# Two half products ordered by row block, attention's own bank marked free a tick later, and GpSimd's last sum moved ahead of its last power

## The chip, the cores and the metric

The kernel runs on one core of a Trainium2 chip. Its time is the device time of one execution in microseconds (us); several executions are timed, and their median counts. A profiled execution is taken beside them, and its trace is what the views below are read from. Engines are named as in the profile: PE is TensorE's matmul, PEld its weight load, DVE is VectorE, ACT is ScalarE, POOL is GpSimd, SP is SyncE, which here only issues transfers.

## The reference

Two decoder layers on 512 rows of 1024 features, in float32. The even layer projects its input into retention heads and an RG-LRU branch, gates both, and maps them back. The odd layer, where the change lies, is differential attention with 8 heads:

```
q, k, v, g = split(h @ w_in);  q, k = rope(q), rope(k)        # two maps a head
p   = softmax(masked q k^T)                                   # by blocks of 128 rows
out = (p[map 0] - lam * p[map 1]) @ v                         # 256 columns a head
out = out * rsqrt(mean(out^2) + eps) * subln_g * (1 - lambda_init) * silu(g)
y   = out @ w_out
h   = layer_norm(alpha * h + y)
```

The result of that last layer norm is the output.

## The kernel before

The 512 rows are four row blocks of 128. Every float32 operand is held as two parts, high and low (`split`: ScalarE rounds the high part, VectorE subtracts it), and every product is three matmuls (`mm3`, line 155: high by high, low by high, high by low) into the same bank of PSUM. Weights come as pieces of 128 x 1024 through `fetch` (line 170): SP issues the load into one of a few raw buffers, ScalarE and VectorE split it into one of five slots of `wsp`. `take(ahead)` (line 191) hands out the next piece and first fetches up to `ahead` pieces beyond it, so a later `take` is also what puts later loads into the program. A slot is free again when PE has read its old piece for the last time, and the cast of the piece five places on waits for that.

**Order.** PE and SP run in program order, as the code is written. The order of DVE, ACT and POOL is planned by the framework from its own estimate of times, with priorities (`tc.high_priority`); a few instructions are pinned by `tc.keep_in_program_order`. Each engine then takes its instructions strictly in that order.

**Ticks.** The attention of a head and row block is a generator (`attention`, line 684) that is mixed into other matmul work by a small planner, `Side` (line 54). After each step of three matmuls the surrounding unit calls `side.tick()`; a tick advances `now` by one and runs at most one piece of one due job, looking at no more than the first three attention jobs in order. A piece ends with `yield n`, due again n ticks later. The pieces of a block are: scores of both maps with their exponentials (`as`, `e`); transposes of the weights into `wt`; the value product into `po` (rows `po<-ov..`), followed by ACT's squares, POOL's sum and power and DVE's `o`; transposes of `o` into the second half of the same bank (rows `L740`), whose copy by ACT and DVE into `om<head>h` and `om<head>l` empties the bank. The waits between them are `ATT_SCORES` (7 or 8 ticks), `ATT_TURN` (3 or 4) and `ATT_NORM` (5), each one more while `busy[0]` is set, in the combined units.

**The bank of the value product.** There is one own bank (`ps_av`). `av[0]` holds the tick from which it counts as free:

```
if own:
    av[0] = side.now + ATT_FREE
```

with `ATT_FREE` = 2, set when the transposes of `o` are issued. In query and key units (`spare[0]` true) a block may instead borrow one of the four banks of the projections (`ps_pj`), once in 8 ticks. Elsewhere it waits for its own bank. If PE reaches a bank that is not emptied yet, PE waits.

**The units of the odd layer** (list `od`, line 307): values and gates of the first two heads, query and key units of heads 0 to 2, then for group g = 1 to 3 a combined unit of gates and values (`gates_values`, line 816), an output unit (`odd_out`, for two heads that are done), and query and key units; at the end the output unit of heads 6 and 7 with the last layer norm. The order is combined unit 1, output of heads 0 and 1, queries and keys of heads 3 and 4, combined unit 2, output of heads 2 and 3, and so on.

**The combined unit** computes gates and values of two heads from 2 x 2 blocks with seven half products instead of eight. A half product (`product`, line 823) covers two row blocks n = 0, 1 (one bank each) and four pieces of the inner dimension kt = 0 to 3, which lie in two weight pieces: eight steps. Its loops run over the weight piece, then the row block, then the two kt of that piece, so a bank gets two steps, the other two, the first two again, and the other the last two. The first half product goes into the banks `one`, the second into `two` (`gv<g>a` and `gv<g>b` in the trace). `copies` (line 834) then copies `one` to SBUF, `gate` (line 840) adds `two` to the copy on DVE. When the unit starts, some of the four banks have just been used by the query and key units or were lent to attention.

**The end.** `layer_norm` (line 397) of row block 2 is `late`: its second half goes over ACT and POOL, in pieces that `odd_end` (line 880) starts through `rest()` while block 3's output is computed. POOL's multiplication is followed by its addition (line 424), which at present is issued from within block 3's norm, right behind its `rsqrt` (the power at line 395) by the hook `then()`. SP sends each half row block out when it is done.

Of the kernel before, what the change touches and what calls it, by code (L numbers as in the profile page):

```python
# [11 lines left out]
ALU = mybir.AluOpType  # L12
# [91 lines left out]
def trunk(ctx: ExitStack, tc: tile.TileContext, a):  # L104
# [38 lines left out]
    def cut(t, *ix):  # L143
        return t[0][ix], t[1][ix]
# [249 lines left out]
    def rsqrt(var, out):  # L394
        nc.gpsimd.tensor_tensor(out=out, in0=var, in1=nhalf[:, :1], op=ALU.pow)  # L395

    def layer_norm(y, sb, gb, late=False, src=None, then=lambda: None):
        hv = [y[:, sb, hf * HALF:hf * HALF + HALF] for hf in range(2)]
        src = [hv[0], src or hv[1]]
        st = stats.pop(sb, None)  # L400
        if st is None:
            st = small.tile([P, 2, 6], F32, tag="bst", name="bst", bufs=2)
            for hf in range(2):
                nc.vector.bn_stats(out=st[:, hf], in_=hv[hf])
        mv = small.tile([P, 2], F32, tag="bmv", name="bmv", bufs=2)
        nc.vector.bn_aggr(out=mv, in_=st)
        rs = small.tile([P, 1], F32, tag="lrs", name="lrs", bufs=2)
        ve = small.tile([P, 1], F32, tag="rs", name="lve")
        nc.vector.tensor_scalar(out=ve, in0=mv[:, 1:2], scalar1=EPS, scalar2=None, op0=ALU.add)  # L409
        rsqrt(ve, rs)  # L410
        then()
        if late:


            nc.vector.scalar_tensor_tensor(out=hv[0], in0=hv[0], scalar=mv[:, 0:1], in1=gb[0][0], op0=ALU.subtract, op1=ALU.mult)
            yield
            nm = small.tile([P, 1], F32, tag="lnm", name="lnm", bufs=1)
            tc.keep_in_program_order(nc.vector.tensor_scalar(out=nm, in0=mv[:, 0:1], scalar1=rs, scalar2=-1.0, op0=ALU.mult, op1=ALU.mult))
            nc.scalar.activation(out=hv[1], in_=hv[1], func=AF.Identity, scale=rs, bias=nm)
            nc.gpsimd.tensor_tensor(out=hv[1], in0=hv[1], in1=gb[0][1], op=ALU.mult)  # L420
            yield
            tc.keep_in_program_order(nc.vector.scalar_tensor_tensor(out=hv[0], in0=hv[0], scalar=rs, in1=gb[1][0], op0=ALU.mult, op1=ALU.add))
            yield 0, hv[0]
            tc.keep_in_program_order(nc.gpsimd.tensor_tensor(out=hv[1], in0=hv[1], in1=gb[1][1], op=ALU.add))
            yield 1, hv[1]
            return
        for hf in range(2):
            nc.vector.scalar_tensor_tensor(out=hv[hf], in0=src[hf], scalar=mv[:, 0:1], in1=gb[0][hf], op0=ALU.subtract, op1=ALU.mult)
        for hf in range(2):
            nc.vector.scalar_tensor_tensor(out=hv[hf], in0=hv[hf], scalar=rs, in1=gb[1][hf], op0=ALU.mult, op1=ALU.add)  # L430
            yield hf, hv[hf]
# [252 lines left out]
    def attention(hd, qb, q, k, m):  # L684
# [57 lines left out]
            split(pm.rearrange("p (i s) -> p i s", s=P), cut(m, ALL, ALL, slice(qb * P, qb * P + P)))  # L742

        if own:
            av[0] = side.now + ATT_FREE

    oj, om, vs, vt, av = {}, {}, {}, {}, [0]

# [67 lines left out]
    def gates_values(i):  # L816
        def block(r, c):
            return lambda kt, n: cut(h, ALL, 4 * c + kt, slice((2 * r + n) * P, (2 * r + n) * P + P))

        def total(k):  # L820
            return lambda kt, n: tuple(sx[:, k, x, kt, n * P:n * P + P] for x in range(2))

        def product(ps, left, start, then=lambda: None):
            for j in range(2):
                if j:
                    then()
                w = take(3)
                for n in range(2):
                    for kt in range(2 * j, 2 * j + 2):
                        c = kt % 2 * HALF  # L830
                        mm3(ps[n], left(kt, n), cut(w, ALL, slice(c, c + HALF)), start and kt == 0, kt == KT // 2 - 1, skip_group_check=not start)
                        side.tick()

        def copies(ps, name, ts):

            for n in range(2):
                ts.append(work(f"{name}{i}{n}"))
                tc.keep_in_program_order(nc.scalar.copy(out=ts[n], in_=ps[n]))

        def gate(ps, ts, r):  # L840
            g = gp.tile([P, 2, S], F32, tag="g", name=f"og{i}{r}")
            for n in range(2):
                for hd in (2 * i - 2, 2 * i - 1):
                    side.need(oj[hd, 2 * r + n])
                gates[2 * r + n, i] = g[:, n]
            for n in range(2):
                nc.vector.tensor_tensor(out=g[:, n], in0=ps[n], in1=ts[n], op=ALU.add)
                silu2(g[:, n], g[:, n], ts[n])

        busy[0] = ATT_BUSY  # L850
        one = [bank(ps_pj, "pj", f"gv{i}a{n}") for n in range(2)]
        two = [bank(ps_pj, "pj", f"gv{i}b{n}") for n in range(2)]
        p1, u, p7, low = [], [], [], []
        product(one, block(0, 0), True)
        copies(one, "p1", p1)
        product(two, block(0, 1), True)
        gate(two, p1, 0)
        product(one, total(0), False)
        copies(one, "u", u)
        product(two, total(1), True, lambda: load_sum(0, 0))  # L860
        copies(two, "p7", p7)
        product(one, total(0), False, lambda: load_sum(3, 1))
        past(i - 1)
        for n in range(2):
            nc.vector.scalar_tensor_tensor(out=p7[n], in0=one[n], scalar=-1.0, in1=p7[n], op0=ALU.mult, op1=ALU.subtract)
            low.append(pair(vp, [P, S], "v", f"ov{i}{2 + n}"))
            split(p7[n], low[n])
        product(two, block(1, 1), False)
        gate(two, u, 1)
        product(one, total(1), False)  # L870
        for n in range(2):
            t = pair(vp, [P, S], "v", f"ov{i}{n}")
            nc.scalar.activation(out=t[0], in_=one[n], func=AF.Identity, scale=-1.0)
            nc.vector.scalar_tensor_tensor(out=t[1], in0=one[n], scalar=-1.0, in1=t[0].bitcast(F32), op0=ALU.mult, op1=ALU.subtract)
            vs.setdefault(i, []).append(t)
        vs[i] += low
        vt[i] = side.now + GV_VALUE
        busy[0] = 0

    def odd_end(sb):  # L880
        nonlocal rest
        last = sb == SB - 1
        norm = layer_norm(y, sb, gb1, sb == SB - 2, residual.get(1) if last else None, (lambda: rest()) if last else (lambda: None))

        def steps():
            for t in norm:
                if t is not None:
                    nc.sync.dma_start(out=a["out"][sb, :, t[0] * HALF:t[0] * HALF + HALF], in_=t[1])
                if sb == SB - 2:
                    yield  # L890

        if sb == SB - 2:
            it = steps()
            next(it)
            rest = lambda: next(it, None)
        else:
            for _ in steps():
                pass

    def past(g):  # L900
        if g >= 0:
# [160 lines left out]
```

## Time and profile before

| | |
|---|---|
| median of the timed runs | 919.15 us (918.99 to 919.6, three runs) |
| profiled execution | 919.45 us, its span 917.7 us |
| granted TensorE clock, mean | 0.998 |
| PE busy | 905.8 us, 99% |
| DVE, ACT, POOL busy | 718.1, 517.6, 113.1 us |
| DMA | 152.93 MB, mean 167 GB/s |

The span runs from the first to the last instruction; the rest of the profiled execution's time lies around it. Times in rows are us from the start of the span. In a timeline row stand the start, the duration, the engine, the line, the operation, the output tile and its inputs, the shape, a count, and in brackets the idle time before it with what ended it. Matmul ends are modelled, so distances between the starts of matmuls say more than their durations. In a row of windows stand the stretch, its length, and the busy time and count of each engine, then clock, DMA share and GB/s.

### The profile page before, as it was taken

The page shows a single profiled execution, that of the slowest core. Times are in us where ns is not written, and L with a number is a line of the kernel's source. Part 1 is how long each engine was busy: PE and PEld are TensorE (multiplying, and loading weights), DVE is VectorE, ACT ScalarE, POOL GpSimd, SP SyncE. Part 2 cuts the span into 40 slices and gives each one's busy share as a digit, 9 for nine tenths or more (in the row PEclk, how much of TensorE's full clock was granted, in tenths as well). Part 3 has the DMA queues.
Part 4 walks back from the last instruction along what each step waited for, and adds up shares of the span by engine and source line. Part 5 has one row for each costly group of instructions (what it writes and reads, how often), then busy time and mean ns, then how long its engine had stood idle before and what let it go on. Part 6 is the DMA issues. An engine that isn't in the chain of part 4 may idle for free.

```text
span 917.7 us, 11876 instructions
## 1 busy us (share of the span) xinstructions
PE 905.8 (99%) x4258; PEld 750.6 (82%) x4258; DVE 718.1 (78%) x1191; ACT 517.6 (56%) x846; POOL 113.1 (12%) x190
## 2 busy tenths in 40 slices
PE   9999999999999999999999999999999999999996
PEld 7888887888888888888888878888888888888885
DVE  5887977958868998897868887748877668867687
ACT  5567787546575668533456666435655355665440
POOL 2311010110102010010101120000120100201112
PEclk9999999999999999999999999999999999999999
DMA  8985463872829471434842226646247382178102
GB/s 288 283 278 149 125 186 91 245 203 58 263 78 270 113 205 51 169 129 149 326 179 70 69 70 229 229 161 252 70 136 250 142 321 92 58 265 276 45 1 92
DMA packets 46524, 152.93 MB, mean 167 GB/s; under 512 B 6145, under 2 KB 6273, under 8 KB 45697
## 3 DMA queue, kind: packets, MB, share of 16 engines
q1 hardware_dynamic: 41472, 135.39, 41.5%
q0 software_dynamic: 4992, 16.78, 9.5%
q8 instruction: 33, 0.54, 0.2%
q14 instruction: 27, 0.21, 0.1%
HBM read 139.57 MB, written 37.75 MB: 193 GB/s over the span
## 4 chain that ended last, share of the span: by engine, by line
PE 87%; DVE 6%; ACT 3%; issue 2%; POOL 1%; DMA 1%; SPq 0%; DVEq 0%; ACTq 0%; POOLq 0%
PE oo_ps L157 8%; PE gr_ps L157 5%; PE out_ps L157 4%; PE q_ps L157 4%; PE gl_ps L157 4%; PE ev_ps L157 4%; PE k_ps L157 4%; PE xb_ps L157 4%; PE po L157 3%; PE as L157 3%; PE ov_ps L157 2%; PE gv3a L157 2%; PE gv2a L157 2%; PE eo_ps L157 2%; PE og_ps L157 2%; PE gv3b L157 2%
## 5 line engine op out<-in xcount | busy, mean ns | idle before, releaser
L697 ACT ACTIVATE e<-as,nm 128x128 f32<-128x128 f32 (+3 forms) x64 | 33.2, 524 | 33.5 <-DVE nm L694 33.3
L704 POOL TENSOR_SCALAR zr<-z 128x1 f32<-128x1 f32 x32 | 16.4, 511 | 248.1 <-ACT e L697 248.1
L736 DVE SCALAR_TENSOR_TENSOR o<-po,ars,og 128x256 f32<-128x256 f32 x32 | 15.5, 484 | 35.0 <-POOL ars L395 35.0
L186 POOL DMA_DIRECT2D t<-t x24 | 19.2, 799 | 160.3 <-DMA t<-in_od_w 157.7
L733 POOL TENSOR_SCALAR ave<-ss,zr 128x1 f32<-128x1 f32 x32 | 16.4, 512 | 141.2 <-ACT po L730 135.2
L186 POOL DMA_DIRECT2D t<-in_od_w x24 | 19.1, 796 | 117.9 <-DMA t<-in_od_w 117.8
L694 DVE CUSTOM_DVE_ANT_0 as<-as,mask 128x128 f32<-128x128 f32 (+3 forms) x64 | 30.4, 506 | 2.3 <-PE as L157 2.3
L730 ACT ACTIVATE po<-po 128x256 f32<-128x256 f32 x32 | 11.9, 371 | 24.6 <-PE po L157 24.4
L575 DVE TENSOR_TENSOR xbp<-xbp,xc 128x512 f32<-128x512 f32 x8 | 5.5, 692 | 17.5 <-ACT xbp L572 17.5
L395 POOL TENSOR_TENSOR ars<-ave,nhalf 128x1 f32<-128x1 f32 x32 | 18.8, 587 | 2.7
L705 DVE SCALAR_TENSOR_TENSOR e<-e,zr,e 128x128 f32<-128x128 f32 (+3 forms) x32 | 17.6, 549 | 0.8
L558 DVE SCALAR_TENSOR_TENSOR xc<-xbp,vecs,xc 128x509 f32<-128x509 f32 (+2 forms) x24 | 17.8, 744 | 0.2
L395 POOL TENSOR_TENSOR lrs<-lve,nhalf 128x1 f32<-128x1 f32 x8 | 7.3, 912 | 83.1 <-DVE lve L409 83.1
L514 DVE TENSOR_TENSOR rsd<-rs,dec 128x512 f32<-128x512 f32 (+3 forms) x32 | 15.5, 484 | 2.1 <-PE rs L157 1.9
L278 DVE TENSOR_TENSOR y<-oo_ps,y 128x512 f32<-128x512 f32 x23 | 15.3, 685 | 2.2 <-PE oo_ps L157 2.1
L567 ACT ACTIVATE t<-pr,vecs 128x512 f32<-128x512 f32 x8 | 5.5, 688 | 17.5 <-PE pr L157 17.4
L709 PE MATMUL wt<-ident,e 128*128 128x128 f32 x80 | 13.9, 272 | 0.0
L152 ACT CAST hh<-ht 128x512 fp32r<-128x512 f32 x8 | 4.7, 588 | 15.5 <-PE ht L654 15.5
L709 PEld LDWEIGHTS wt<-ident,e 128*128 128x128 f32 x80 | 10.5, 140 | 3.4
L583 ACT ACT_TABLE_LOAD x8 | 10.3, 1283 | 4.2 <-DVE xc L582 4.1
L702 DVE RECIPROCAL zr<-z 128x1 f32<-128x1 f32 x32 | 5.2, 162 | 9.6 <-ACT e L697 9.4
L697 ACT ACTIVATION_READ_ACCUMULATOR e<-as,nm 128x1 f32 x64 | 12.5, 195 | 0.0
(2844 smaller groups left out, 3478.0 us busy)
## 6 DMA issues: line engine op xcount, KB each, us to landing
w_r<-in_od_w SPq DMA_DIRECT2D x58, 512.0 KB, 5.9
w_r<-in_ev_w SPq DMA_DIRECT2D x47, 512.0 KB, 5.1
t<-in_od_w SPq DMA_DIRECT2D x48, 256.0 KB, 5.5
sx<-sd SPq DMA_DIRECT2D x24, 512.0 KB, 5.7
w_r<-t SPq DMA_DIRECT2D x24, 512.0 KB, 3.3
w_r<-in_ev_wo SPq DMA_DIRECT2D x16, 512.0 KB, 4.5
w_r<-in_od_wo SPq DMA_DIRECT2D x16, 512.0 KB, 4.7
t<-in_od_w POOLq DMA_DIRECT2D x24, 256.0 KB, 5.2
```

What stands on the lines that cost most here:

```text
L157: nc.tensor.matmul(out=out, lhsT=l[n == 2], rhs=r[n == 1], start=start and n == 0, stop=stop and n == 2, **kw)
L186: nc.gpsimd.dma_start(out=dst, in_=two, max_dma_last_dim=4 * D, accum_op=ALU.add)
L395: nc.gpsimd.tensor_tensor(out=out, in0=var, in1=nhalf[:, :1], op=ALU.pow)
L514: nc.vector.tensor_tensor(out=s[:, :n], in0=ps[:, :n], in1=dec[:, :n], op=ALU.mult)
L558: nc.vector.scalar_tensor_tensor(out=xc[:, sh:], in0=xb[:, :S - sh], scalar=conv_w(w, c), in1=xc[:, sh:], op0=ALU.mult, op1=ALU.add)
L694: nc.vector.tensor_tensor_reduce(out=ps[:, :n], in0=ps[:, :n], in1=mask[:, S - n:], scale=-QK_SCALE, scalar=3.0e38, op0=ALU.add, op1=ALU.m ...
L697: nc.scalar.activation(out=e, in_=ps[:, :n], func=AF.Exp, scale=-1.0, bias=nm, accum_out=z[:, mp:mp + 1])
L704: nc.gpsimd.tensor_scalar(out=zr[:, 1:2], in0=z[:, 0:1], scalar1=z[:, 0:1], scalar2=EPS, op0=ALU.mult, op1=ALU.mult)
L705: nc.vector.scalar_tensor_tensor(out=ee[0], in0=ee[1], scalar=zr[:, 0:1], in1=ee[0], op0=ALU.mult, op1=ALU.add)
L709: nc.tensor.transpose(out=pt[:, kb * P:kb * P + P], in_=ee[0][:, kb * P:kb * P + P], identity=ident)
L733: nc.gpsimd.tensor_scalar(out=ve, in0=ss, scalar1=zr[:, 1:2], scalar2=None, op0=ALU.add)
L736: nc.vector.scalar_tensor_tensor(out=o, in0=po[:, :2 * P], scalar=rs, in1=gates[qb, hd // 2][:, hc:hc + 2 * P], op0=ALU.mult, op1=ALU.mult)
```

## The change

In `gates_values` the first two half products get `apart=True`: both weight pieces are taken first, and then all four steps of row block 0 are issued before those of row block 1. The number of steps, ticks and matmuls is the same.

In `attention` the own bank counts as free one tick later (3 instead of 2) when the transposes are issued outside query and key units.

In `layer_norm` POOL's addition follows its multiplication at once, before block 3's norm begins; the hook `then` is gone, and `odd_end` sends both halves of block 2 one after the other.

```
--- before.py
+++ after.py
@@ -394,7 +394,7 @@
     def rsqrt(var, out):
         nc.gpsimd.tensor_tensor(out=out, in0=var, in1=nhalf[:, :1], op=ALU.pow)
 
-    def layer_norm(y, sb, gb, late=False, src=None, then=lambda: None):
+    def layer_norm(y, sb, gb, late=False, src=None):
         hv = [y[:, sb, hf * HALF:hf * HALF + HALF] for hf in range(2)]
         src = [hv[0], src or hv[1]]
         st = stats.pop(sb, None)
@@ -408,7 +408,6 @@
         ve = small.tile([P, 1], F32, tag="rs", name="lve")
         nc.vector.tensor_scalar(out=ve, in0=mv[:, 1:2], scalar1=EPS, scalar2=None, op0=ALU.add)
         rsqrt(ve, rs)
-        then()
         if late:
 
 
@@ -418,11 +417,10 @@
             tc.keep_in_program_order(nc.vector.tensor_scalar(out=nm, in0=mv[:, 0:1], scalar1=rs, scalar2=-1.0, op0=ALU.mult, op1=ALU.mult))
             nc.scalar.activation(out=hv[1], in_=hv[1], func=AF.Identity, scale=rs, bias=nm)
             nc.gpsimd.tensor_tensor(out=hv[1], in0=hv[1], in1=gb[0][1], op=ALU.mult)
+            nc.gpsimd.tensor_tensor(out=hv[1], in0=hv[1], in1=gb[1][1], op=ALU.add)
             yield
             tc.keep_in_program_order(nc.vector.scalar_tensor_tensor(out=hv[0], in0=hv[0], scalar=rs, in1=gb[1][0], op0=ALU.mult, op1=ALU.add))
-            yield 0, hv[0]
-            tc.keep_in_program_order(nc.gpsimd.tensor_tensor(out=hv[1], in0=hv[1], in1=gb[1][1], op=ALU.add))
-            yield 1, hv[1]
+            yield from enumerate(hv)
             return
         for hf in range(2):
             nc.vector.scalar_tensor_tensor(out=hv[hf], in0=src[hf], scalar=mv[:, 0:1], in1=gb[0][hf], op0=ALU.subtract, op1=ALU.mult)
@@ -742,7 +740,7 @@
             split(pm.rearrange("p (i s) -> p i s", s=P), cut(m, ALL, ALL, slice(qb * P, qb * P + P)))
 
         if own:
-            av[0] = side.now + ATT_FREE
+            av[0] = side.now + ATT_FREE + (not spare[0])
 
     oj, om, vs, vt, av = {}, {}, {}, {}, [0]
 
@@ -820,7 +818,16 @@
         def total(k):
             return lambda kt, n: tuple(sx[:, k, x, kt, n * P:n * P + P] for x in range(2))
 
-        def product(ps, left, start, then=lambda: None):
+        def product(ps, left, start, then=lambda: None, apart=False):
+            if apart:
+
+                ws = [take(3) for _ in range(2)]
+                for n in range(2):
+                    for kt in range(KT // 2):
+                        c = kt % 2 * HALF
+                        mm3(ps[n], left(kt, n), cut(ws[kt // 2], ALL, slice(c, c + HALF)), kt == 0, kt == KT // 2 - 1)
+                        side.tick()
+                return
             for j in range(2):
                 if j:
                     then()
@@ -851,9 +858,9 @@
         one = [bank(ps_pj, "pj", f"gv{i}a{n}") for n in range(2)]
         two = [bank(ps_pj, "pj", f"gv{i}b{n}") for n in range(2)]
         p1, u, p7, low = [], [], [], []
-        product(one, block(0, 0), True)
+        product(one, block(0, 0), True, apart=True)
         copies(one, "p1", p1)
-        product(two, block(0, 1), True)
+        product(two, block(0, 1), True, apart=True)
         gate(two, p1, 0)
         product(one, total(0), False)
         copies(one, "u", u)
@@ -879,23 +886,18 @@
 
     def odd_end(sb):
         nonlocal rest
-        last = sb == SB - 1
-        norm = layer_norm(y, sb, gb1, sb == SB - 2, residual.get(1) if last else None, (lambda: rest()) if last else (lambda: None))
+        norm = layer_norm(y, sb, gb1, sb == SB - 2, residual.get(1) if sb == SB - 1 else None)
 
         def steps():
             for t in norm:
-                if t is not None:
+                if t is None:
+                    yield
+                else:
                     nc.sync.dma_start(out=a["out"][sb, :, t[0] * HALF:t[0] * HALF + HALF], in_=t[1])
-                if sb == SB - 2:
-                    yield
-
-        if sb == SB - 2:
-            it = steps()
-            next(it)
-            rest = lambda: next(it, None)
-        else:
-            for _ in steps():
-                pass
+
+        it = steps()
+        rest = lambda: next(it, None)
+        rest()
 
     def past(g):
         if g >= 0:
```

## The prediction

> **What bounds the kernel now.** I read the page first, then the waits of TensorE (PE), then windows, then timelines around each place that the change touches.
>
> ```profile
> span 917.7 us, 11876 instructions
> PE 905.8 (99%) x4258; PEld 750.6 (82%) x4258; DVE 718.1 (78%) x1191; ACT 517.6 (56%) x846; POOL 113.1 (12%) x190
> ...
> PE 87%; DVE 6%; ACT 3%; issue 2%; POOL 1%; DMA 1%; SPq 0%; DVEq 0%; ACTq 0%; POOLq 0%
> ```
>
> PE is busy for 99% of the span and carries 87% of the chain that ended last. Its matmul work is not changed in number, so only two things can move the time: moments in which PE stands still, and the tail after its last matmul. The waits of PE, the rows that lie where the change works:
>
> ```profile
> PE gv1a L157 <- DVE om1l L153: 0.4, 1, 0.4
> ...
> PE po L157 <- DVE om1l L153: 0.2, 1, 0.2
> ...
> PE po L157 <- DVE om4l L153: 0.2, 1, 0.2
> ```
>
> They are tenths of a microsecond each. Idle time understates them, because a matmul's modelled end lies after the start of the next one; so I size every stall by the distance between starts. The whole stake of the change is a few such stalls, in a kernel where 0.2% (about what a measurement of this kernel can tell from no change) is 1.84 us.
>
> **Part 1, the first two half products block by block.** The windows that hold exactly these two products, for groups 1, 2 and 3, with the same 82 or 81 matmuls and transposes in each:
>
> ```profile
> 532.33:548.90 16.57, 15.95 (x82) 12.74 (x81) 13.32 (x29) 10.49 (x23) 3.81 (x6) 1.00 0.20 65
> 657.37:672.74 15.37, 15.37 (x82) 12.89 (x80) 13.29 (x29) 11.26 (x24) 5.54 (x6) 1.00 0.21 69
> 780.74:796.11 15.37, 15.37 (x81) 12.89 (x80) 13.30 (x29) 11.26 (x24) 5.54 (x6) 1.00 0.21 69
> ```
>
> Group 1 takes 1.20 us more than the other two. The timeline of PE shows where:
>
> ```profile
> 533.25 0.39 PE L157 MATMUL gv1a<-w84l,hh 128*128 128x512 f32 x1
> 533.47 0.39 PE L157 MATMUL gv1a<-w84h,hl 128*128 128x512 f32 x1
> 534.27 0.50 PE L157 MATMUL gv1a<-w84h,hh 128*128 128x512 f32 x1 [0.41 <-DVE om1l L153]
> 534.61 0.40 PE L157 MATMUL gv1a<-w84l,hh 128*128 128x512 f32 x1
> ...
> 542.71 0.40 PE L157 MATMUL gv1b<-w86h,hl 128*128 128x512 f32 x1
> 543.31 0.51 PE L157 MATMUL gv1b<-w86h,hh 128*128 128x512 f32 x1 [0.20 <-DVE om1l L153]
> 543.66 0.40 PE L157 MATMUL gv1b<-w86l,hh 128*128 128x512 f32 x1
> ```
>
> Undisturbed matmuls of 512 columns start 0.22 to 0.23 us apart. At 534.27 the distance is 0.80, and the next is 0.34: 0.57 + 0.11 = 0.69 lost with rounding. At 543.31 it is 0.60 and then 0.35: 0.37 + 0.12 = 0.49. Sum 1.18, which is the 1.20 of the windows. Both come at the third step of a half product (a step is three matmuls, one tick), the first one on the second row block's bank, and both wait for `om1l`: that bank was lent to attention's head 1, and VectorE is still copying the lent block out.
>
> With `apart` the second block is first written in the fifth step, two steps (2 x 3 x 0.23 = 1.38 us) later, with attention's insertions after the same ticks as before. In the first product it would be wanted at 533.47 + 0.23 + 1.38 = 535.08 where the bank is free by 534.27: a margin of 0.8. In the second, at 542.71 + 0.23 + 1.38 = 544.32, or 543.63 with the first stall gone; free by 543.31 even if the copy does not move up with PE. I take the whole of it, **-1.18**. Groups 2 and 3 have no such stall and gain nothing: bounds 0 to -1.18 for the part by itself.
>
> What it moves: the second weight block is wanted two steps sooner, and it had been cast before the product began: VectorE's timeline has no cast of `w85` or `w87` in these windows, nor of their like in groups 2 and 3. Fetching both at once puts one weight load on SP's queue, and its two casts, four ticks earlier in the program; nothing else stands on SP's queue between the two places. The cost can lie at the other end: the first weight block of each product is now read until the sixth step instead of the fourth, and a cast five blocks on waits for its slot:
>
> ```profile
> 535.97 1.06 ACT L152 CAST w89h<-w_r 128x1024 fp32r<-128x1024 f32 x1 [0.45 <-PE gv1a L157]
> ```
>
> ScalarE takes its work in order, so while this cast waits (two steps, 1.38 us more) what is queued behind it, copies of attention's transposed blocks, waits too, and behind them PE. The order of ScalarE and VectorE is planned by the framework, which will mostly put ready work ahead. Groups 2 and 3 show what there is to spare:
>
> ```profile
> 547.12 1.21 DVE L153 TENSOR_TENSOR w91l<-w_r,w91h 128x1024 fp32r<-128x1024 f32 x1
> ...
> 548.71 0.68 DVE L847 TENSOR_TENSOR og<-gv1b,p 128x512 f32<-128x512 f32 x1
> ...
> 550.88 0.42 DVE L153 TENSOR_TENSOR om1l<-po,om1h 128x256 fp32r<-128x256 f32 x1
> ...
> 672.21 0.42 DVE L153 TENSOR_TENSOR om3l<-po,om3h 128x256 fp32r<-128x256 f32 x1
> ```
>
> ```profile
> 550.75 0.39 PE L157 MATMUL gv1a<-w88h,sx 128*128 128x512 f32 x1
> 551.35 0.39 PE L157 MATMUL po<-ov00h,w13h 128*128 128x256 f32 x1 [0.22 <-DVE om1l L153]
> 551.58 0.28 PE L157 MATMUL po<-ov00l,w13h 128*128 128x256 f32 x1
> ...
> 674.10 0.28 PE L157 MATMUL po<-ov10h,w33h 128*128 128x256 f32 x1
> ```
>
> In group 2 the copy ends at 672.63, 1.47 us before PE's next value product at 674.10: that is the cover. In group 1 it ends at 551.30 and PE waits; the stall is (0.60 - 0.23) + (0.23 - 0.12) = 0.48, with 0.12 the pace of these narrow matmuls (below). The later tick of part 2 does not reach it: this product is due five ticks after its own transposes of the weights (`ATT_TURN` 4 and `ATT_BUSY` 1), which is after the bank's due time in either version. Part 1 pulls on it both ways. The gate's first sum (0.68, at 548.71, ahead of the copy) has its bank complete two steps sooner and can leave the stretch: -0.68. The cast `w91l` reads the slot of the second product's first weight block and goes up to 1.38 later: it ends 0.34 after the transposes at 547.99 now and would end about 1.0 after, +0.7. I take 0 for this stall, with -0.48 and +1.38 as bounds.
>
> **Part 2, the own bank free a tick later outside the query and key units.**
>
> ```profile
> 547.99 0.38 PE L740 MATMUL po<-ident,o 128*128 128x128 f32 x2
> ...
> 594.51 0.38 PE L740 MATMUL po<-ident,o 128*128 128x128 f32 x2
> ...
> 595.88 0.40 PE L157 MATMUL oo_ps<-w98h,om0l 128*128 128x512 f32 x1
> 596.44 0.39 PE L157 MATMUL po<-ov10h,w22h 128*128 128x256 f32 x1 [0.16 <-DVE om2l L153]
> 596.66 0.28 PE L157 MATMUL po<-ov10l,w22h 128*128 128x256 f32 x1
> 596.78 0.28 PE L157 MATMUL po<-ov10h,w22l 128*128 128x256 f32 x1
> ...
> 598.30 0.60 PE L709 MATMUL wt<-ident,e 128*128 128x128 f32 x4
> ```
>
> In an output unit the due time decides: transposes out of the own bank at 594.51, two steps, and the next value product at 596.44, where PE waits (0.56 - 0.23) + (0.22 - 0.12) = 0.43. A third step puts 0.69 between, more than the 0.33 by which the copy was late. The second output unit shows the same wait on `om4l`, so 2 x 0.43: **-0.86**, bounds 0 to -0.86. The blocks of a head slip by one, two and three ticks through the unit; the last one's transposes slip into the next query unit, where no other attention work is queued, since the next head's blocks start only when its keys are done. In the last output units one slip moves the chain of head 7 by a tick; its last transposes come two ticks into the third row block's output, and the fourth, which reads them, is six ticks on.
>
> What is late next: the output products of the unit's second half take over the banks of the first half, and the last of these is emptied by this:
>
> ```profile
> 596.30 0.68 DVE L276 SCALAR_TENSOR_TENSOR y<-y,oo_ps 128x512 f32<-128x512 f32 x1
> ```
>
> It ends at 596.98. The step that needs this bank starts at present behind the four transposes of 598.30, at about 598.7. With the value product moved behind it (its wait of 0.33, one matmul of 0.22, eight of 0.12: 1.5) that becomes about 597.2. Some 0.2 of cover is left, so I cost it at nothing; with the cover gone it is up to 0.43 a unit, the gain itself.
>
> **Part 3, GpSimd's sum ahead of its last power.** VectorE and GpSimd in the tail:
>
> ```profile
> 910.97 0.74 DVE L428 SCALAR_TENSOR_TENSOR y<-y,bmv,ln 128x512 f32<-128x512 f32 x1
> 911.63 0.74 DVE L428 SCALAR_TENSOR_TENSOR y<-oo_ps,bmv,ln 128x512 f32<-128x512 f32 x1
> 912.29 2.27 DVE L430 SCALAR_TENSOR_TENSOR y<-y,lrs,ln 128x512 f32<-128x512 f32 x2
> ...
> 909.35 1.45 POOL L420 TENSOR_TENSOR y<-y,ln 128x512 f32<-128x512 f32 x1 [1.25 <-ACT y L419]
> 911.20 0.92 POOL L395 TENSOR_TENSOR lrs<-lve,nhalf 128x1 f32<-128x1 f32 x1 [0.40 <-DVE lve L409]
> 912.09 1.26 POOL L424 TENSOR_TENSOR y<-y,ln 128x512 f32<-128x512 f32 x1
> ```
>
> ```profile
> DMA to landing us min/median/max: 2.0/2.0/2.2
> ```
>
> The pair at L430 takes 2.27 where the pair at L428 takes 1.40 (910.97 to 912.37): 0.87 more, while the sum runs (912.09 to 913.35). Moved, the sum runs from 910.80 (the end of the product) to 912.06; the power, queued behind it on GpSimd, ends at 912.98 instead of 912.12, and L430, which waits for it, starts 0.86 later and takes 0.87 less: nothing. If the pair at L428 is held up by the sum instead, it ends at 913.24 and L430 at +0.1. If the sum takes 1.45 like the product, +0.2. The output of the sum no longer leaves between the last transfers, whose landing takes 2.0 to 2.2: -0.1 or -0.2. I take **-0.1**, bounds -0.2 to +0.3. The order of the outputs on SP's queue stays.
>
> [...]
>
> Sum: -1.18 - 0.86 - 0.1 = -2.14. The profiled execution took 919.45 (span 917.7 and 1.75 around it), 0.30 above the median; 919.45 - 2.14 = 917.3 for it and 919.15 - 2.14 = **917.0** for the median.
>
> **The rivals.**
> (a) The wait at 551.35 goes as well: for it speaks that VectorE's gate sum can leave the stretch, against it the later cast. 917.0 - 0.48 = 916.5.
> (b) One pair of stalls comes back in another shape: in the output units at the bank emptied at 596.98 (for it: 0.2 of cover; against: that copy may run ahead of the later `om2l`), or in the half products. 0.86 or 1.18 less: 917.9 to 918.2.
> (c) Slower than before: the weight casts that wait two steps longer stand ahead of attention's copies, in every group. If ScalarE's 1.06 and VectorE's 1.21 both precede the copy, groups 2 and 3 lose 2.27 - 1.47 = 0.80 each, and group 1, without cover, the two steps, 1.38: 2.98 - 2.14 = +0.84, so 920.0. It decides once the casts cost over 0.7 a group. Against it: attention's copies have priority in the plan.
> (d) The change doesn't do what it says: new small waits eat the gain, since a matmul order fixed by hand meets a plan of the other engines made anew; 919.1.
>
> **How the numbers follow.** Chances: forecast 0.46 (its own range 916.6 to 917.5), (a) 0.20, (b) 0.18, (c) 0.09, (d) 0.07. Faster by over 0.2% means below 917.31: three quarters of the forecast and all of (a), 0.54. Slower, above 920.99: a third of (c) and a little for what I don't foresee, 0.05. The rest, 0.41, is within. The range 916.2 to 918.8 holds all but (c), most of (d) and the far end of (a).
>
> **What would show it.** The window of the first two products in group 1 takes 15.4 instead of 16.6, and no PE row there names `om1l`; no value product in an output unit names `om2l` or `om4l`; GpSimd's rows in the tail read product, sum, power, and L430's pair takes 1.4. Wrong would be: a PE wait on a `w..l` cast or on `y`, a stall at `w33` or `w53`, or a last power that ends after 913.2 less the gain.

## The result, and the profile after

The changed kernel is slower: median 923.63 us (923.38 to 925.42, five runs) beside 919.6 us (918.99 to 920.04) for the kernel before, ratio 1.0047 with a 95% interval of 1.0036 to 1.0058. The profiled execution took 923.38 us, its span 921.4, that is 3.7 more than the 917.7 before. Where these 3.7 us lie is told by cutting both spans at the starts of the same matmuls (the first of each unit, and the last of all; in us, a negative difference is a gain):

| stretch | before | after | difference |
|---|---|---|---|
| start of the span to combined unit 1 | 532.33 | 532.02 | -0.31 |
| combined unit 1 | 48.54 | 52.10 | +3.56 |
| output units 0 and 1 with their query and key units | 76.50, 76.51 | 76.08, 76.08 | -0.42, -0.43 |
| combined units 2 and 3 | 46.86, 46.86 | 47.69, 47.69 | +0.83, +0.83 |
| query and key unit before the last output | 28.01 | 27.97 | -0.04 |
| last output unit to its last matmul | 53.88 | 53.79 | -0.09 |
| last matmul to the end | 8.17 | 7.94 | -0.23 |

The sum is +3.70. The first row is no part of the change: nothing before unit 1 is touched, and over all the kernels below this stretch lies between 531.62 and 532.33. The output and query units, the end and the tail gain; the three combined units lose 5.2.

The page of the changed kernel:

```profile
span 921.4 us, 11877 instructions
PE 906.6 (98%) x4258; PEld 752.2 (82%) x4258; DVE 718.9 (78%) x1191; ACT 516.1 (56%) x846; POOL 108.3 (12%) x190
PE 82%; DVE 9%; ACT 3%; issue 3%; POOL 2%; DMA 0%; DVEq 0%; SPq 0%; ACTq 0%; POOLq 0%
```

The busy times have hardly moved. The chain that ended last has: VectorE's share in it is 9% where it was 6%, PE's 82% where it was 87%. The waits of PE:

```profile
PE po L157 <- DVE om1l L153: 3.1, 1, 3.1
...
PE po L157 <- DVE om3l L153: 0.6, 1, 0.6
PE po L157 <- DVE om5l L153: 0.6, 1, 0.6
```

All the rows that the prediction set out to remove are gone: none names `om1l` at `gv1a` or `gv1b`, none `om2l` or `om4l`. In their place stand three others, one in each combined unit, at the value products that read `w13`, `w33` and `w53`. The first had been 0.2 before; the other two had not been there. Windows of the changed kernel, first the two half products of groups 1 and 2 (busy time and count of PE, PEld, DVE, ACT, POOL, then the granted clock), then the stretch that holds the wait at `w13` and the one behind it:

```profile
532.02:547.68 15.66, 15.61 (x82) 12.82 (x81) 11.66 (x23) 9.21 (x21) 3.69 (x6) 1.00 0.18 61
660.20:675.57 15.37, 15.37 (x81) 12.89 (x80) 13.06 (x29) 10.52 (x24) 3.77 (x6) 1.00 0.20 69
...
549.69:553.11 3.42, 0.32 (x2) 0.13 (x2) 3.27 (x8) 2.76 (x6) 0.28 (x1) 1.00 0.00 0
553.11:556.52 3.41, 3.41 (x15) 3.22 (x16) 2.15 (x3) 1.11 (x3) 0.04 (x1) 0.50 0.00 0
```

The half products of group 1 take 15.66 instead of 16.57: 0.91 of the 1.20 over the other groups is gone; group 2's 15.37 is what it was. The other two rows show what came instead. PE is busy for only 0.32 us of the 3.42 before 553.11, and in the 3.41 us after that its granted clock is 0.50. PE's timeline there, and at the same product of group 2:

```profile
549.50 0.39 PE L157 MATMUL gv1a<-w88h,sx 128*128 128x512 f32 x1
552.99 0.49 PE L157 MATMUL po<-ov00h,w13h 128*128 128x256 f32 x1 [3.10 <-DVE om1l L153]
553.27 0.41 PE L157 MATMUL po<-ov00l,w13h 128*128 128x256 f32 x1
553.49 0.41 PE L157 MATMUL po<-ov00h,w13l 128*128 128x256 f32 x1
...
555.62 0.63 PE L157 MATMUL gv1a<-w88h,sx 128*128 128x512 f32 x1
556.04 0.62 PE L157 MATMUL gv1a<-w88l,sx 128*128 128x512 f32 x1
...
677.69 0.39 PE L157 MATMUL po<-ov10h,w33h 128*128 128x256 f32 x1 [0.60 <-DVE om3l L153]
```

By distances of starts PE waits 552.99 - 549.50 - 0.23 = 3.26 at `w13`, where the kernel before waited 0.37. Then the narrow matmuls start 0.21 to 0.22 apart instead of 0.12, and the first wide ones 0.42. The twelve narrow ones take 555.62 - 552.99 = 2.63; in the run with the undisturbed clock that is shown below they take 1.53. The six wide ones behind them take 1.81 instead of 6 x 0.23. That is 1.10 + 0.43 = 1.53 us for the slow clock. So combined unit 1 loses 2.89 by the wait and 1.53 by the clock and gains 0.91: +3.51, of the +3.56 measured.

What the copy `om1l` waits for is on ScalarE and VectorE. ScalarE before, where the cast of `w91` is done before the exponentials `e`:

```profile
545.00 1.05 ACT L152 CAST w91h<-w_r 128x1024 fp32r<-128x1024 f32 x1
548.69 0.37 ACT L697 ACTIVATE e<-as,nm 128x128 f32<-128x128 f32 x1 [2.64 <-DVE nm L694]
...
549.40 0.58 ACT L152 CAST w13h<-wt 128x512 fp32r<-128x512 f32 x1
...
550.39 0.38 ACT L152 CAST om1h<-po 128x256 fp32r<-128x256 f32 x1
```

ScalarE after:

```profile
548.48 0.63 ACT L811 ACTIVATE p<-og 128x512 f32<-128x512 f32 x1 [3.09 <-DVE og L854]
549.02 0.35 ACT L695 ACTIVATE e<-as,nm 128x128 f32<-128x128 f32 x1
...
549.70 1.04 ACT L152 CAST w91h<-w_r 128x1024 fp32r<-128x1024 f32 x1
550.63 0.59 ACT L152 CAST w13h<-wt 128x512 fp32r<-128x512 f32 x1
551.11 0.39 ACT L152 CAST om1h<-po 128x256 fp32r<-128x256 f32 x1
...
674.98 1.06 ACT L152 CAST w117h<-w_r 128x1024 fp32r<-128x1024 f32 x1
675.93 0.38 ACT L152 CAST om3h<-po 128x256 fp32r<-128x256 f32 x1
```

And VectorE after, with the tail at its end:

```profile
547.70 0.68 DVE L854 TENSOR_TENSOR og<-gv1b,p 128x512 f32<-128x512 f32 x1
...
550.77 1.23 DVE L153 TENSOR_TENSOR w91l<-w_r,w91h 128x1024 fp32r<-128x1024 f32 x1
551.91 0.68 DVE L153 TENSOR_TENSOR w13l<-wt,w13h 128x512 fp32r<-128x512 f32 x1
552.52 0.41 DVE L153 TENSOR_TENSOR om1l<-po,om1h 128x256 fp32r<-128x256 f32 x1
...
676.08 1.22 DVE L153 TENSOR_TENSOR w117l<-w_r,w117h 128x1024 fp32r<-128x1024 f32 x1
677.22 0.42 DVE L153 TENSOR_TENSOR om3l<-po,om3h 128x256 fp32r<-128x256 f32 x1
...
914.89 1.50 DVE L426 SCALAR_TENSOR_TENSOR y<-y,bmv,ln 128x512 f32<-128x512 f32 x1
916.31 0.74 DVE L426 SCALAR_TENSOR_TENSOR y<-oo_ps,bmv,ln 128x512 f32<-128x512 f32 x1
916.98 1.40 DVE L428 SCALAR_TENSOR_TENSOR y<-y,lrs,ln 128x512 f32<-128x512 f32 x2
```

Before, VectorE's half `w91l` stood at 547.12, ahead of the gate's sum and of attention's work. Now the cast pair of `w91` stands between the exponentials `e` and the copies of `w13` and `om1`, on both engines. The gate's first sum (547.70) and its Tanh (548.48) have moved too, ahead of the exponentials. In group 2 it is `w117` that stands ahead of `om3`.

How late the slot is can be read from PE. The slot of `w91` holds `w86`, which PE reads for the last time here:

```profile
545.12 0.40 PE L157 MATMUL gv1b<-w86h,hl 128*128 128x512 f32 x1
```

Before the change, that last read started at 544.58 and the cast at 545.00. So the slot is free at about 545.5 now, and ScalarE then stands idle until 548.48 (the 3.09 in the row of the Tanh); the cast runs at 549.70 all the same. From the start of the unit, the slot comes 0.85 later than before and the cast 5.01. In group 2 the last read of `w112`, whose slot `w117` takes, comes 2.50 later, and the cast 3.31.

The new waits leave two readings open: the weight casts that come later ("theory 2" in the expectations below), or the gate's first sum and Tanh that come earlier ("theory 1"). Counted from the first matmul of unit 1, three times tell what each does: when the copy of the bank ends, when PE would reach `w13`, and when it starts it.

### The profile page after: what moved, and what is told of

Read it like the earlier page. It is cut to its first block, busy times and chain, and to the rows that moved or that the text cites. A ratio compares the mean times of both kernels' runs of the same rounds, so it can differ in the third digit from the quotient of the medians.

```text
span 921.4 us, 11877 instructions
## 1 busy us (share of the span) xinstructions
PE 906.6 (98%) x4258; PEld 752.2 (82%) x4258; DVE 718.9 (78%) x1191; ACT 516.1 (56%) x846; POOL 108.3 (12%) x190
## 4 chain that ended last, share of the span: by engine, by line
PE 82%; DVE 9%; ACT 3%; issue 3%; POOL 2%; DMA 0%; DVEq 0%; SPq 0%; ACTq 0%; POOLq 0%
PE oo_ps L157 10%; PE ev_ps L157 5%; PE gr_ps L157 5%; PE out_ps L157 4%; PE q_ps L157 4%; PE gl_ps L157 4%; PE k_ps L157 4%; PE xb_ps L157 4%; PE po L157 2%; PE ov_ps L157 2%; PE eo_ps L157 2%; PE og_ps L157 2%; PE as L157 2%; PE gv3a L157 2%; PE gv2a L157 2%
## 5 line engine op out<-in xcount | busy, mean ns | idle before, releaser
L702 POOL TENSOR_SCALAR zr<-z 128x1 f32<-128x1 f32 x32 | 12.6, 394 | 247.8 <-ACT e L695 247.8
L738 PEld LDWEIGHTS po<-ident,o 128*128 128x128 f32 x64 | 8.9, 140 | 4.6 <-DVE o L734 0.5
```

## The experiments

"Wait" is the time PE lost at the start of the product that reads `w13`, from starts of matmuls; each ratio is to runs of the kernel before that were taken beside it. Their medians were 919.6 for the changed kernel, 919.34 for the next four, 919.54 for the three after them and 919.23 for the last.

| kernel | median, us | ratio to before | unit 1 | copy ends | PE due | wait |
|---|---|---|---|---|---|---|
| before | | | 48.54 | 18.97 | 18.64 | 0.37 |
| changed | 923.63 | 1.0047 | 52.10 | 20.91 | 17.71 | 3.26 |
| no half product apart | 918.15 | 0.9988 | 48.51 | 18.93 | 18.57 | 0.42 |
| first apart only | 919.0 | 0.9998 | 49.46 | 19.85 | 18.40 | 1.50 |
| second apart only | 921.87 | 1.0025 | 51.63 | 20.77 | 18.09 | 2.73 |
| changed, Tanh held back | 922.54 | 1.0032 | 51.61 | 20.64 | 17.71 | 2.99 |
| changed, casts held back | 919.53 | 0.9998 | 49.30 | 19.68 | 17.78 | 1.95 |
| changed, both held back | 918.55 | 0.9986 | 48.95 | 19.37 | 17.75 | 1.69 |
| old order, casts held back | 917.62 | 0.9977 | 48.09 | 17.87 | 18.64 | 0 |
| changed, all three casts out of the way | 917.56 | 0.9985 | 47.99 | 17.75 | 17.46 | 0.34 |

**Parts 2 and 3 without part 1.**

```
-        product(one, block(0, 0), True, apart=True)
+        product(one, block(0, 0), True)
-        product(two, block(0, 1), True, apart=True)
+        product(two, block(0, 1), True)
```

> The changed kernel with both half products in their old order; the later tick and the moved sum stay. All theories agree that the half products carry the whole loss. Then the two waits in output units (0.43 us each) are gone, the tail is 0.24 us shorter as in the profile of the change, and the stalls of the first product rows (0.69 and 0.49 us on om1l) and at w13 (0.48) are back: 919.6 - 0.86 - 0.24 = 918.5 us. If part of the loss were in the later tick, it would stay above 919.6.

918.15 us (917.55 to 919.0), ratio 0.9988 (0.9979 to 0.9997): 1.2 us faster. The stages of its profile give 0.44 and 0.43 for the output units with their query and key units, 0.03 for unit 1, 0.03 for the last stretches before the tail and 0.22 for the tail: 1.15. The combined units keep their old stalls. So the whole loss comes with part 1, and parts 2 and 3 keep what they gained.

**One half product at a time.** First the change with only the first half product apart, then with only the second.

```
-        product(two, block(0, 1), True, apart=True)
+        product(two, block(0, 1), True)
```

> Only the first half product goes block by block, the second has its old order. Theory 1 (the gate's first Tanh, ready two steps sooner in the plan, is put ahead of the exponentials and of the copy of the weights on ScalarE, and holds them until VectorE has made the gate's sum): nothing of the loss, the 0.69 us stall gone, the 0.49 us stall and the w13 stall of 0.48 us as before the change: 918.5 - 0.7 = 917.8 us. Theory 2 (the casts that wait two steps longer for their slot stand ahead of attention's copies): the cast of w89 is late here too, so part of the loss at w13 stays, 1 us or more, and the time is 919 us or above.

919.0 us, ratio 0.9998 (0.9989 to 1.0007). The stall in the first half product (0.69) is gone, but the one in the second grows from 0.37 to 0.84 at its first distance, and the wait at `w13` is 1.50. In groups 2 and 3 there is no wait at `w33` or `w53`.

```
-        product(one, block(0, 0), True, apart=True)
+        product(one, block(0, 0), True)
```

> Only the second half product goes block by block. Theory 1: nearly the whole loss is here: w13 waits about 3 us, w33 and w53 0.8 us each, about 923 us. Theory 2: the cast of w89 is not late here, that of w91 is; about half of the loss, 921 us, with ScalarE's wait spent on a cast and not on the Tanh.

921.87 us, ratio 1.0025 (1.0016 to 1.0035). The wait at `w13` is 2.73, and at `w33` and `w53` it is 0.26 + 0.10 each. The granted clock is again 0.50 for 3.41 us, from before PE resumes at 552.74:

```profile
552.16:555.57 3.41, 2.83 (x13) 2.83 (x14) 2.85 (x5) 0.67 (x2) 0.00 (x0) 0.50 0.00 0
```

The second half product does most of the damage. It is its first weight piece whose slot the cast of `w91`, `w117` or `w143` waits for.

**The gate's first Tanh held back.** The full change, with the first Tanh of a gate kept in its place in the program, so that the framework can't move it ahead.

```
-        nc.scalar.activation(out=t, in_=x, func=AF.Tanh, scale=0.5)
+        act = nc.scalar.activation(out=t, in_=x, func=AF.Tanh, scale=0.5)
+        if pin:
+            tc.keep_in_program_order(act)
...
-                silu2(g[:, n], g[:, n], ts[n])
+                silu2(g[:, n], g[:, n], ts[n], r == 0)
```

> The changed kernel with one thing more: the Tanh of the first gate stays in program order on ScalarE, that is behind attention's work issued before it. The late casts of w89 and w91 stay as they are in the change. Theory 1: the stalls at w33 and w53 vanish and w13's falls from 3.3 to 0.5 us or less, and the time is 917.0 to 917.5 us. Theory 2: the casts still stand ahead, w13 waits over 2 us, and the time stays above 921 us.

922.54 us, ratio 1.0032 (1.002 to 1.0045). The copy ends 0.27 sooner and the wait is 2.99; at `w33` and `w53` 0.57 + 0.10 are left of 0.76 + 0.11. The clock falls to 0.50 here too. So the Tanh has a share of 0.3 in the lateness of the copy, and does not carry it.

**The casts held back.** The full change, with the cast pair of one weight piece in each group (`w91`, `w117`, `w143`) kept in its place in the program, behind attention's copies.

```
+    pinned = set()
...
+                if n in pinned:
+                    tc.keep_in_program_order(nc.scalar.copy(out=w[0][:, c], in_=raw[:, c]))
+                    tc.keep_in_program_order(nc.vector.tensor_tensor(out=w[1][:, c], in0=raw[:, c], in1=w[0][:, c].bitcast(F32), op=ALU.subtract))
+                    yield
+                    continue
...
         gate(two, p1, 0)
+        pinned.add(taken[0] + 3)
         product(one, total(0), False)
```

> The changed kernel with one thing more: both casts of w91, w117 and w143 (the piece five on from the second half product's first) stay in program order on ScalarE and VectorE, which puts them behind the copies of attention's weights and of its bank. The Tanh stays ahead as in the change. Theory 2 (the casts): the pair's 1.06 and 1.2 us leave the chain to the value product, the waits at w33 and w53 (0.87 each with the slower first matmuls) vanish, that at w13 falls from 3.3 to about 2.1 us: 919.2 us if PE's slow stretch behind the long wait goes with it, 920.7 if not. Theory 1 (the Tanh): no change, 923.6 us.

919.53 us, ratio 0.9998 (0.9989 to 1.0007): 4 us of the changed kernel's time are gone with one pair of casts a group. ScalarE, and then PE, in this kernel:

```profile
549.45 0.58 ACT L152 CAST w13h<-wt 128x512 fp32r<-128x512 f32 x1
549.92 0.39 ACT L152 CAST om1h<-po 128x256 fp32r<-128x256 f32 x1
...
552.56 1.03 ACT L181 CAST w91h<-w_r 128x1024 fp32r<-128x1024 f32 x1
```

```profile
551.44 0.39 PE L157 MATMUL po<-ov00h,w13h 128*128 128x256 f32 x1 [1.79 <-DVE om1l L153]
...
552.85 0.28 PE L157 MATMUL po<-ov03h,w13l 128*128 128x256 f32 x1
```

The copies stand directly behind the exponentials, and the cast behind them. The waits at `w33` and `w53` are gone altogether: in groups 2 and 3 the cast was the whole of the loss. In group 1 the copy ends 1.23 sooner, PE idles 1.79, and the twelve narrow matmuls take 552.85 + 0.12 - 551.44 = 1.53. The granted clock there is undisturbed:

```profile
551.44:555.30 3.86, 3.86 (x24) 3.44 (x25) 2.91 (x4) 3.28 (x6) 0.27 (x1) 1.00 0.02 3
```

But 1.95 of wait is left in group 1, and part 1 is still no gain over the first experiment.

**Both held back.** The edits of the last two together. The times are of one run of this kernel, the profile is of a second one.

> Both pins together: the Tanh of the first gate and the casts of w91 and its like behind attention's copies; the block order of both half products stays as in the change. Theory 2: 0.3 to 0.5 us under the run with the casts alone pinned, 918.5 to 919 us, w13 still waiting 1.5 us or more. Theory 3 (in group 1 a chain over ScalarE, GpSimd and VectorE sets when the value product w13 can start, and PE time saved in front of it is waited for there): no gain from the block order at all, 918.5 us or above, not below the next run. If the 1.18 us of the two removed stalls were PE's own to keep, it would be 916.5 us.

> The kernel with both pins once more, for its profile. From the times of the runs before: the copy of attention's bank that w13 waits for ends 19.4 us after the first matmul of group 1's half products (20.9 in the change, 19.7 with the casts alone pinned, 17.9 with the old block order and the casts pinned), while PE is at w13 17.7 us after it: a wait of about 1.7 us is left.

918.55 us, ratio 0.9986 (0.9977 to 0.9995); the profiled execution of the second run took 918.05. The copy ends at 19.37, another 0.31 sooner. The copy is then still 0.40 later than before the change, although PE is due 0.89 earlier; the wait is 1.69. The lateness of the copy by 1.94 is so made up of 1.23 (cast), 0.31 (Tanh) and 0.40 (the rest).

**The old order with the casts held back.** Parts 2 and 3, no half product apart, and the casts kept behind the copies.

> Old order of both half products, the later tick and the moved sum, and the casts of w91 and its like behind attention's copies. Theory 2: the cast of w91 stood 1.2 us long on VectorE ahead of the copy that w13 waits for even before the change, so that wait of 0.48 us goes: 917.7 us. Theory 3: the same. If the casts don't matter: 918.2 us, as without the pin.

917.62 us (917.16 to 918.23), ratio 0.9977 (0.9968 to 0.9986). This beats both kernels; by ratio it is the best of the study. The rows that it leaves:

```profile
PE gv1a L157 <- DVE om1l L153: 0.4, 1, 0.4
...
PE gv1b L157 <- DVE om1l L153: 0.2, 1, 0.2
```

These are the two stalls that part 1 was made for. They are still there, and yet unit 1 takes 48.09 instead of 48.54, since the copy ends at 17.87, 0.77 ahead of PE, and the wait at `w13` is gone.

**All three casts out of the way.** The half products apart, Tanh and `w91` held back, and the casts of `w89` and `w90` moved behind attention's squares and copies as well, by a later second `take` (the second half product gets `late=True`; the loads behind it are issued later too):

```
-                ws = [take(3) for _ in range(2)]
+                ws = [take(2)] if late else [take(3) for _ in range(2)]
                 for n in range(2):
                     for kt in range(KT // 2):
+                        if kt // 2 == len(ws):
+                            pinned.add(taken[0] + 2)
+                            ws.append(take(2))
...
-        product(two, block(0, 1), True, apart=True)
+        product(two, block(0, 1), True, apart=True, late=True)
         gate(two, p1, 0)
+        pinned.update((taken[0] + 2, taken[0] + 3))
         product(one, total(0), False)
```

> Block order of both half products as in the change, the Tanh and the casts of w91 pinned, and two casts more out of the way: that of w89 behind the squares of w12's value product on ScalarE, that of w90 behind the copies for w13 (their loads are issued four to eight ticks later for it). Theory 2 and 3 together: the chain gets shorter by one cast on ScalarE (0.95) and one on VectorE (1.14), to about 17.5 us after the first matmul, PE is at w13 after 17.7 and hardly waits, and the 1.18 us of the block order are kept: 917.6 - 1.2 = 916.4 us, the fastest of all. If the block order itself lengthened the chain in another way than through the casts and the Tanh, the time would stay at 917.6 us or above.

917.56 us, ratio 0.9985 (0.9976 to 0.9994), 1.2 us above what was expected and, by the intervals, not to be told from the run before. The copy ends at 17.75, 1.62 sooner than with both held back; no stall is left in the half products and 0.34 at `w13`. But unit 1 takes 47.99, only 0.10 less than in the old order. PE's waits and the timelines of VectorE and GpSimd (line numbers of this kernel are a few higher) show why:

```profile
PE po L744 <- DVE o L740: 0.4, 1, 0.4
```

```profile
552.18 1.23 DVE L182 TENSOR_TENSOR w90l<-w_r,w90h 128x1024 fp32r<-128x1024 f32 x1 [0.24 <-ACT w90h L181]
553.32 1.22 DVE L182 TENSOR_TENSOR w91l<-w_r,w91h 128x1024 fp32r<-128x1024 f32 x1
554.46 1.22 DVE L153 TENSOR_TENSOR w92l<-w_r,w92h 128x1024 fp32r<-128x1024 f32 x1
556.52 0.48 DVE L740 SCALAR_TENSOR_TENSOR o<-po,ars,og 128x256 f32<-128x256 f32 x1 [0.85 <-POOL ars L401]
...
554.53 1.30 POOL L737 TENSOR_SCALAR ave<-ss,zr 128x1 f32<-128x1 f32 x1 [6.40 <-DVE w91l L182]
555.92 0.57 POOL L401 TENSOR_TENSOR ars<-ave,nhalf 128x1 f32<-128x1 f32 x1
```

The three casts, 3.67 us by their durations, now run one behind the other ahead of the next block's `o`. They are not the last link: VectorE is done with them at 555.68 and then idles 0.85 for GpSimd's power. GpSimd's sum before it takes 1.30, where the mean in this kernel is 0.49, and ends 0.16 after `w92l`; in the old order with the casts held back it takes 1.11 and ends 0.16 after `w92l` as well. So in both the sum ends only behind the last cast, and `o` follows it. Counted from the start of the unit, `o` ends at 24.80 instead of 24.40 in the old order, and PE is due at its transposes at 24.31 instead of 25.02: PE waits 0.55 by distances. The stalls removed in front have come back further on a third time.

Not tried: one more slot for the weights, which would take the wait for the slot itself away.

## Why the prediction was wrong

**Part 1, the two stalls.** Predicted -1.18 in the window of the half products; -0.91 came, with both stalls gone. The mechanism and the margins (0.8 and more) were right. The prediction then put these 1.18 into the sum as a gain of time. That is the first thing that failed: PE arrived 0.93 earlier at `w13` (17.71 instead of 18.64) and had to wait there for a copy that did not come earlier. The old stalls had stood in front of a wait that was already there, 0.48 by the quoted rows. Removing them could only be worth what the chain behind that wait gave back. The run with the first product apart shows the same between the two stalls: the first removed, the second grows by 0.47.

**The term that failed most** is "I take 0 for this stall, with -0.48 and +1.38 as bounds". The wait grew by 2.89, beyond both bounds, by two causes that the prediction had separately and did not add: PE is 0.93 earlier, and the copy 1.94 later. The copy's lateness was bounded by the two steps that the slot is released later, +1.38. That was the wrong measure. In group 1 the slot comes only 0.85 later and would have left ScalarE time for the cast before the exponentials; the cast loses its place in ScalarE's and VectorE's order. Before, both halves of `w91` were done ahead of the exponentials. After, they stand between these and the copies, and cost a whole cast, 1.23. In group 2 the two steps hold attention's matmuls too, and the slot comes 2.50 later, not 1.38. The gate's sum and Tanh, which the prediction let "leave the stretch" for -0.68, did move up, but ahead of attention's chain; holding the Tanh back gained 0.27 to 0.31.

**The cover in groups 2 and 3.** The prediction took the 1.47 there to be enough, since attention's copies would have priority. Rival (c) had the case right that came: ScalarE's 1.06 and VectorE's 1.21 both ahead of the copy, "2.27 - 1.47 = 0.80 each". The copy `om3l` ends 677.64 - 660.20 = 17.44 after the unit's start instead of 672.63 - 657.37 = 15.26, 2.18 later, and 0.83 a unit came. With the casts held back it is 0. Rival (c) had a chance of 0.09. Against it stood that "attention's copies have priority in the plan": the code does give them a high priority, but no row showed that this keeps a weight cast behind them, and it does not. The row of `w89h` quoted there already showed such a cast waiting 0.45 for its slot on ScalarE, ahead of other work. For group 1 rival (c) had +1.38, too little for the reasons above, and it had no slow clock.

**The slow clock,** 1.53 us in group 1 at a granted clock of 0.50, stood in no term and no rival. It goes with the long wait and is not a separate cause of the lateness: with the wait at 1.95 the granted clock is 1.00.

**Part 2** came out as argued: -0.86 predicted, -0.42 and -0.43 measured. No row names `om2l` or `om4l`, and the bank emptied at 596.98 made no new wait. Two of the eight transposes of `o` in each output unit slip into the query and key units behind it, as the prediction said of the last block. So the output units go from 28.72 to 28.05 and the query and key units from 47.77 to 48.03: part of the saving is only moved, and some 0.42 is left.

**Part 3** was predicted at -0.1, with bounds of -0.2 and +0.3; -0.23 came, a little beyond. GpSimd's rows read product, sum, power:

```profile
913.04 1.46 POOL L419 TENSOR_TENSOR y<-y,ln 128x512 f32<-128x512 f32 x1 [1.24 <-ACT y L418]
914.58 1.26 POOL L420 TENSOR_TENSOR y<-y,ln 128x512 f32<-128x512 f32 x1
915.80 0.99 POOL L395 TENSOR_TENSOR lrs<-lve,nhalf 128x1 f32<-128x1 f32 x1
```

The last pair (line 428 now) takes 1.40 where it took 2.27, and the first instruction of the pair before it (line 426) 1.50 where it took 0.74, while the sum runs from 914.58 to 915.84. The loss of 0.76 moved from one pair to the other, where most of it is hidden: the last pair could not begin before the power ends, at 916.79, and begins at 916.98. VectorE's last instruction ends 4.96 after the start of the last matmul instead of 5.06; the other 0.13 comes behind it, where the transfers land in a median of 2.0 as before. So of the cases that the prediction left open, the one came in which the pair before is held up by the sum, with 0.76 lost there where it reckoned 0.87; but the last pair ended 0.10 sooner, not the 0.1 later of that case.

**The sum.** Predicted -1.18 + 0 - 0.86 - 0.1 = -2.14. Measured for the same parts, in spans: unit 1 +3.56 instead of -1.18, units 2 and 3 +1.66 instead of 0, the output and query units -0.85, the end and the tail -0.36. That is +4.01, less the 0.31 by which the part before the change differed between the two executions.

**What stays open.** Which estimate makes the framework put the cast of `w91` ahead of the copies was not examined; shown is that its place in the order carries the loss in group 1, since the slot was free 4 us before the cast; in groups 2 and 3 the later slot and the place were not told apart. The 0.40 of lateness left with both held back is gone with all three casts out of the way, so it is put down to `w89` and `w90`; that kernel also issues loads later, and which of these it is was not told apart.

## What to carry to other kernels

A stall of the bounding engine is worth removing only as far as the next wait downstream has slack: find the next instruction that waits for work of an in-order chain on other engines, and ask whether that chain moves up too. An edit that holds a buffer longer should be costed by the place in the in-order queues that its refill takes, the whole instruction on each engine, and not by the time it is held: in group 1 a cast of 1.23 us, where the slot came 0.85 later. Here one cast pair moved behind the copies brought 0.42 us in unit 1 in the old order (48.51 to 48.09); removing both stalls of the half products on top of that, with the Tanh and two more casts moved for it, brought 0.10.

## What the runs showed of the hardware that was not expected

Three long waits of PE cost more than their length. After PE had idled 3.10, 2.83 and 2.57 us at `w13` (the change, the Tanh held back, the second product alone), the granted clock was 0.50 for 3.41 us, the same each time; the row of the run with the Tanh held back:

```profile
552.51:555.92 3.41, 3.14 (x13) 3.06 (x14) 3.15 (x5) 0.99 (x3) 0.00 (x0) 0.50 0.00 0
```

After 1.79, 1.53 and 1.34 us (the casts held back, both held back, the first product alone) it stayed at full speed: the granted clock behind the wait was 1.00 in the first and the third, and in the second unit 1 less its wait took 47.26 us, beside 47.35 in the first. In the run with the second product alone the clock had already fallen at 552.16, when PE had been idle for 2.0 us. With the Tanh held back it fell at 552.51, 2.6 us after PE had gone idle, and in the changed kernel at 553.11, 3.2 us after. So in these six waits the longest idling that left the clock alone is 1.79 us, and the shortest by which it had fallen is 2.0; whether it also depends on when the wait falls, no run tells apart. By the distances of the eighteen matmuls behind the wait it added 1.53, 1.40 and 1.25 us, less where part of the slow 3.41 us had passed before PE resumed.

One execution of the kernel with both held back took 1841.24 us; the other ten lie between 918.34 and 919.43. Its page shows PE busy for 1831.4 us with the same 4258 matmuls, while VectorE's busy time, 741.6 us, is close to its usual 719. The granted clock is given as 1.000, but its page has no row of the clock, as all the others have, so that figure is no measurement. The matmuls of 512 columns start mostly 0.44 to 0.45 us apart there (1080.05, 1080.49), like those at a clock of 0.50 in the changed kernel (0.42 and 0.43). Why is not known.
